# A hybrid decoder block on one core: the borrowed rows of two recurrence gates, copied by ScalarE instead of subtracted by VectorE

## The chip, the cores and the metric

The kernel runs on one core of a Trainium2 chip. The metric is the device time of one execution in microseconds (us), the median of three runs. One further execution was profiled by the hardware; its page and trace are what this document reads.

## The reference, cut to what matters

A block of 512 positions and 1024 channels is computed in float32. One projection `h @ w_in` yields five parts. One part goes through a gated causal convolution of 31 taps, another through a causal convolution of 4 taps, which yields `xb` with 1280 channels, and then through a gated linear recurrence (RG-LRU). Both results are merged, projected and followed by a SwiGLU feed-forward network. The part around the change is the recurrence:

```python
xh = xf.reshape(bsz, s, LRU_HEADS, LRU_BLOCK)          # 16 heads of 80 channels
r = sigmoid(einsum('bshi,hij->bshj', xh, wa).reshape(bsz, s, d) + ba)
i = sigmoid(einsum('bshi,hij->bshj', xh, wx).reshape(bsz, s, d) + bx)
log_a = -LRU_C * r * softplus(-lam)
a, mult = exp(log_a), sqrt(-expm1(2.0 * log_a))
_, h = associative_scan(combine, (a, mult * (i * xf)), axis=1)
```

The 16 heads are 80 channels wide and the tiles of the kernel are 128 channels wide, so a tile of gate outputs needs input rows of a neighbouring tile.

## The kernel before, in words

Channels lie on the 128 partitions and the 512 positions along the free axis. To reach float32 accuracy every matmul operand is split in two: a **rounded part** `h` (a copy into the type fp32r) and a **low part** `l`, which is the value minus `h`. A product is then three matmuls, `h*h`, `h*l` and `l*h`. The helper `split_to` does this: the copy is ScalarE's (L123), the subtraction (the helper `sub`, L119) is VectorE's for activations and GpSimd's for most weights.

Weights arrive in chunks through SyncE's DMA queue; a chunk is loaded some four chunks before TensorE uses it (`AHEAD`), rounded by ScalarE and subtracted by GpSimd into one of five `hl` buffers.

The middle of the kernel follows a list written out by hand (`ORDER`). Its tokens name steps: `u3` (a tile of the gated convolution's input), `rx3` (`xb3` and its split), `g3` (the two gates of tile 3), `r3` (the recurrence of tile 3), `rg3`, `gb3`, `ga3` (other parts of the projection). Between the steps, `run_beside` emits pieces of the long 31-tap convolution, one VectorE instruction per tap and tile (`cv`, L682), which fill VectorE. Within an engine the program then runs in the order that a scheduler settled by its own costs; what is listed below as an order is its outcome.

The step `rx(j)` ends with `ext_in(j)`, which collects the borrowed rows for the gates that need rows of tile j. For gates 0 and 5 (`j5 == 0`) these are the first 32 rows of `xb1` and of `xb6`. They go into a tile `ext` of 96 rows as rounded, low and rounded part, so that one matmul with 96 rows, against weights stacked in the same way, does all three products. ScalarE writes rows 0 to 31 (L782) and 64 to 95 (L783) from `xb`, and VectorE writes rows 32 to 63 by a subtraction (L784, shown in the trace at the helper's line L119). For the other gates, DMAs copy the rows out of the split parts (L789).

The step `gates(j)` (matmuls at L809) multiplies three pairs of the tile's own rows and then, for even `j5`, the one pair with `ext`. In names of the trace, `g` is a bank of gate sums, `z` a bank of the projection, `hl_in` and `hl_gate` split weights, `mu` a bank that the recurrence uses, `ows` sums of weights for a later stage that GpSimd makes in passing, and `y1` a product for the output of the recurrence.

Of the kernel before, what the change touches and what calls it, by code (L numbers as in the profile page):

```python
# [8 lines left out]
F32 = mybir.dt.float32  # L9
# [29 lines left out]
FEW, MANY = 32, 112  # L39
# [47 lines left out]
def tile_block(ctx, tc, a, out):  # L87
# [15 lines left out]
    def pairt(name, dtype=F32R):  # L103

        return longt(f"{name}h", dtype), longt(f"{name}l", dtype)
# [7 lines left out]
    vec, act, pe, pool_e = nc.vector, nc.scalar, nc.tensor, nc.gpsimd  # L113
# [4 lines left out]
    def sub(eng, o, x, y):  # L118
        return eng.tensor_tensor(out=o, in0=x, in1=y, op=ALU.subtract)  # L119
# [505 lines left out]
    ab, e, s, s2, po, c4 = (sm[:, i, :] for i in range(6))  # L625
# [125 lines left out]
    xb, xbp = [], []  # L751

    def rx(j):
        ps = in_mm(RX + j)
        act.activation(ps, ps, AF.Identity, bias=b_in(RX + j))
        o = longt(f"xb{j}")
        lw = lambda s: pc("lru_conv_w", (KL - 1 - s) * NR + j)
        act.activation(o, ps, AF.Identity, scale=lw(0), bias=pc("lru_conv_b", j))
        for s in range(1, KL):
            vec.scalar_tensor_tensor(out=o[:, s:], in0=ps[:, : T - s], scalar=lw(s), in1=o[:, s:], op0=ALU.mult, op1=ALU.add)  # L760
        xb.append(o)
        p_ = pairt(f"xb{j}")
        split(f"xb{j}", o, vec, p_)
        xbp.append(p_)
        ext_in(j)
# [3 lines left out]
    ext = {}  # L769

    def ext_in(i):
        g5, i5 = i - i % 5, i % 5
        for j5 in range(5):
            for at_, nr, tl, r0 in pieces[j5][1]:
                if tl != i5:
                    continue
                key = g5 + j5
                if key not in ext:
                    ext[key] = pairt(f"ext{key}") if j5 % 2 else (longt(f"ext{key}", F32R),)
                if j5 == 0:  # L780
                    full, e = xb[i][:FEW, :], ext[key][0]
                    act.copy(e[:FEW, :], full)  # L782
                    act.copy(e[2 * FEW : 3 * FEW, :], full)  # L783
                    sub(vec, e[FEW : 2 * FEW, :], full, e[:FEW, :].bitcast(F32))  # L784
                    continue
                src = [v[r0 : r0 + nr, :].bitcast(F32) for v in xbp[i]]
                places = [(0, at_, 0), (1, at_, 1)] if j5 % 2 else [(0, at_ + FEW * k, k % 2) for k in range(3)]
                for d, at0, k in places:
                    nc.sync.dma_start(ext[key][d][at0 : at0 + nr, :].bitcast(F32), src[k])  # L789
# [471 lines left out]
```

## Time and profile before

| what | value |
|---|---|
| runs of the kernel | 802.47 us median of 3 (802.31 to 802.84) |
| profiled execution, own time | 803.2 us |
| its span, first to last instruction | 801.4 us |
| granted TensorE clock, mean | 0.998 |
| TensorE matmul busy | 789.4 us, 99% of the span |
| VectorE busy | 677.3 us, 85% |
| ScalarE busy | 471.5 us, 59% |
| GpSimd busy | 232.3 us, 29% |

A row of a timeline reads: start in us, duration in us, engine, line, operation, what is written `<-` what is read, shape, count, and in brackets the idle time of the engine before it with what ended it. PE is TensorE, DVE is VectorE, ACT is ScalarE, POOL is GpSimd, SP is SyncE. The list of waits gives, for an engine and the work that waited, whom it waited for, then total us, times and the longest. The chain that ended last goes back from the last instruction, at each step to what released it.

### The profile page before, as it was taken

The page shows a single profiled execution, that of the slowest core. Times are in us where ns is not written, and L with a number is a line of the kernel's source. Part 1 is how long each engine was busy: PE and PEld are TensorE (multiplying, and loading weights), DVE is VectorE, ACT ScalarE, POOL GpSimd, SP SyncE. Part 2 cuts the span into 40 slices and gives each one's busy share as a digit, 9 for nine tenths or more (in the row PEclk, how much of TensorE's full clock was granted, in tenths as well). Part 3 has the DMA queues.
Part 4 walks back from the last instruction along what each step waited for, and adds up shares of the span by engine and source line. Part 5 has one row for each costly group of instructions (what it writes and reads, how often), then busy time and mean ns, then how long its engine had stood idle before and what let it go on. Part 6 is the DMA issues. An engine that isn't in the chain of part 4 may idle for free.

```text
span 801.4 us, 12193 instructions
## 1 busy us (share of the span) xinstructions
PE 789.4 (99%) x4374; PEld 689.4 (86%) x4374; DVE 677.3 (85%) x1029; ACT 471.5 (59%) x676; POOL 232.3 (29%) x182
## 2 busy tenths in 40 slices
PE   8999999999999999999999999999999999999997
PEld 7988888788888888888888888999999999888885
DVE  4699999999989988795897889977878887889756
ACT  7546585888668864572335574555455555577443
POOL 3565867686865855130000000000000000000000
PEclk9999999999999999999999999999999999999999
DMA  6946556477564664358948536477655553676652
GB/s 207 242 122 166 163 160 198 128 219 209 169 201 145 194 201 140 116 186 265 287 159 249 172 107 183 113 177 185 159 132 133 133 132 104 202 266 204 197 171 105
DMA packets 184624, 140.29 MB, mean 175 GB/s; under 512 B 14279, under 2 KB 162163, under 8 KB 184563
## 3 DMA queue, kind: packets, MB, share of 16 engines
q1 hardware_dynamic: 183123, 134.27, 55.8%
q0 software_dynamic: 1440, 5.24, 3.5%
q8 instruction: 34, 0.56, 0.3%
q14 instruction: 27, 0.22, 0.1%
HBM read 113.79 MB, written 18.64 MB: 165 GB/s over the span
## 4 chain that ended last, share of the span: by engine, by line
PE 84%; DVE 8%; ACT 3%; DMA 2%; issue 1%; POOL 1%; SPq 0%; ACTq 0%; POOLq 0%; DVEq 0%
PE z L523 29%; PE or L935 13%; PE ft L1062 7%; PE yb L523 7%; PE fa L1062 6%; PE ya L523 5%; PE mxr L935 5%; PE fe L1062 3%; PE fr L1062 3%; DVE cv L682 2%; PE fb L1062 2%; PE g L809 2%; PE f L523 1%; DMA raw_fb<-in_ffn_w_dram 1%; DMA raw_in<-in_w_in_dram 1%
## 5 line engine op out<-in xcount | busy, mean ns | idle before, releaser
L682 DVE SCALAR_TENSOR_TENSOR cv<-u,par,cv 128x511 f32<-128x511 f32 (+16 forms) x240 | 162.1, 729 | 2.7 <-ACT cv L679 2.5
L119 POOL TENSOR_TENSOR hl_in<-raw_in,hl_in 128x1024 fp32r<-128x1024 f32 x52 | 126.0, 2429 | 81.3 <-ACT hl_in L123 77.1
L349 POOL DMA_DIRECT2D raw_fb<-raw_fb x10 | 8.7, 875 | 299.7 <-DVE raw_fb L351 186.9
L119 POOL TENSOR_TENSOR ows<-ows 128x256 f32<-128x256 f32 x66 | 57.1, 867 | 37.6 <-DMA ows<-in_ffn_w_dram 34.7
L123 ACT CAST hl_in<-raw_in 128x1024 fp32r<-128x1024 f32 x52 | 54.2, 1043 | 11.5 <-PE z L523 6.6
L123 ACT CAST hl_ft<-raw_fb 128x1024 fp32r<-128x1024 f32 x40 | 41.9, 1049 | 28.5 <-DVE raw_fb L351 12.4
L119 DVE TENSOR_TENSOR hl_ft<-raw_fb,hl_ft 128x1024 fp32r<-128x1024 f32 x40 | 48.6, 1218 | 9.5 <-ACT hl_ft L123 9.4
L119 DVE TENSOR_TENSOR hl_fb<-raw_fb,hl_fb 128x1024 fp32r<-128x1024 f32 x30 | 36.6, 1220 | 8.6 <-ACT hl_fb L123 8.5
L523 PE MATMUL z<-h10h,hl_in 128*128 128x512 f32 (+1 forms) x112 | 42.2, 378 | 1.2 <-DVE h10l L567 1.2
L523 PE MATMUL z<-h16h,hl_in 128*128 128x512 f32 (+1 forms) x112 | 41.7, 374 | 0.0
L523 PE MATMUL z<-h14h,hl_in 128*128 128x512 f32 (+1 forms) x112 | 41.7, 374 | 0.0
L523 PE MATMUL z<-h11h,hl_in 128*128 128x512 f32 (+1 forms) x112 | 41.7, 374 | 0.0
L523 PE MATMUL z<-h13h,hl_in 128*128 128x512 f32 (+1 forms) x112 | 41.7, 374 | 0.0
L523 PE MATMUL z<-h15h,hl_in 128*128 128x512 f32 (+1 forms) x112 | 41.7, 374 | 0.0
L523 PE MATMUL z<-h17h,hl_in 128*128 128x512 f32 (+1 forms) x112 | 41.7, 374 | 0.0
L523 PE MATMUL z<-h12h,hl_in 128*128 128x512 f32 (+1 forms) x112 | 41.7, 374 | 0.0
L351 DVE TENSOR_TENSOR raw_fb<-raw_fb,raw_fb 128x1024 f32<-128x1024 f32 x20 | 24.5, 1224 | 18.0 <-DMA raw_fb<-in_ffn_w_dram 17.6
L119 DVE TENSOR_TENSOR hl_ob<-raw_ob,hl_ob 128x1024 fp32r<-128x1024 f32 (+1 forms) x23 | 27.0, 1174 | 10.2 <-ACT hl_ob L123 10.2
L123 ACT CAST hl_ob<-raw_ob 128x1024 fp32r<-128x1024 f32 (+1 forms) x23 | 23.3, 1013 | 20.9 <-PE or L935 10.8
L123 ACT CAST hl_fb<-raw_fb 128x1024 fp32r<-128x1024 f32 x30 | 31.4, 1046 | 7.0 <-PE mxr L935 3.7
L1062 PE MATMUL fe<-hs_0h,hl_ft 128*128 128x256 f32 x160 | 30.8, 284 | 0.4 <-DVE hl_ft L119 0.4
L1062 PE MATMUL ft<-hs_1h,hl_ft 128*128 128x256 f32 x160 | 30.4, 283 | 0.0
(964 smaller groups left out, 2611.4 us busy)
## 6 DMA issues: line engine op xcount, KB each, us to landing
raw_in<-in_w_in_dram SPq DMA_DIRECT2D x52, 512.0 KB
raw_fb<-in_ffn_w_dram SPq DMA_DIRECT2D x96, 256.0 KB
ows<-in_ffn_w_dram SPq DMA_DIRECT2D x44, 256.0 KB
os<-ows SPq DMA_DIRECT2D x22, 512.0 KB
raw_ob<-in_ffn_w_dram SPq DMA_DIRECT2D x33, 256.0 KB
raw_ot<-os SPq DMA_DIRECT2D x33, 256.0 KB
raw_lo<-in_lru_w_out_dram SPq DMA_DIRECT2D x16, 320.0 KB
raw_fb<-raw_fb POOLq DMA_DIRECT2D x10, 512.0 KB, 4.6
```

The costliest lines, as they stand in the source:

```text
L119: return eng.tensor_tensor(out=o, in0=x, in1=y, op=ALU.subtract)
L123: copy(h, full)
L349: pool_e.dma_start(out=q, in_=y, accum_op=ALU.add)
L351: vec.tensor_tensor(out=q, in0=q, in1=y, op=ALU.add)
L523: pe.matmul(ps, l, r, start=i == 0, stop=i == n - 1)
L682: vec.scalar_tensor_tensor(out=acc[c][:, s:], in0=u[c][:, : T - s], scalar=dw(c, s), in1=acc[c][:, s:], op0=ALU.mult, op1=ALU.add)
L809: pe.matmul(ps, l, r, start=k == 0, stop=k == len(mms) - 1)
L935: pe.matmul(banks[i], l_[:, ts], r_, start=start and n == 0, stop=stop and n == 2, skip_group_check=again)
L1062: pe.matmul(ps[:, HALVES[i]], lw[:, 4 * i + c, :], rx_, start=not (again or i or c or m), stop=bool(i and c == 3 and m == 2), skip_group_c ...
```

## The change

The low part of `xb1` and of `xb6` exists already in full height as `xb1l` and `xb6l` (VectorE's L119 in `rx`). The change takes rows 32 to 63 of `ext` from there by a copy, so VectorE's subtraction of 32 x 512 goes away, twice, and ScalarE has three copies of 32 x 512 in place of two, twice. The two old copies now also read the rounded part `xb1h` or `xb6h` in place of `xb1` or `xb6`.

```diff
                 if j5 == 0:
-                    full, e = xb[i][:FEW, :], ext[key][0]
-                    act.copy(e[:FEW, :], full)
-                    act.copy(e[2 * FEW : 3 * FEW, :], full)
-                    sub(vec, e[FEW : 2 * FEW, :], full, e[:FEW, :].bitcast(F32))
+                    for n, part in enumerate((0, 1, 0)):
+                        act.copy(ext[key][0][FEW * n : FEW * (n + 1), :], xbp[i][part][:FEW, :].bitcast(F32))
                     continue
```

The scheduler answers with another order on VectorE and ScalarE; TensorE's and GpSimd's orders stay as they were. All lines behind the change are two smaller (L847 is L845 now).

On ScalarE, at the rows for gate 5 (`ext_1547`), before:

```order
L123 CAST xb6h<-xb_1538 128x512
L123 CAST hl_in_1620<-raw_in_1618 128x1024
L782 CAST ext_1547<-xb_1538 32x512
L783 CAST ext_1547<-xb_1538 32x512
L123 CAST y1h<-z_1565 128x512
```

and now:

```order
L123 CAST xb6h<-xb_1538 128x512
L123 CAST hl_in_1620<-raw_in_1618 128x1024
L782 CAST ext_1547<-xb6h 32x512
L782 CAST ext_1547<-xb6l 32x512
L782 CAST ext_1547<-xb6h 32x512
L123 CAST y1h<-z_1565 128x512
```

The copy of the low part stands between the other two, behind nothing new; the cast of `y1h` moves back by one row.

On VectorE, some 8 us ahead of that place, at the gate step of tile 4 (`g` and `ea` are its sums and its decay, `cv` two tiles of the convolution), before:

```order
L682 SCALAR_TENSOR_TENSOR cv_1236<-u_875,par,cv_1236 128x490
L682 SCALAR_TENSOR_TENSOR cv_1238<-u_1112,par,cv_1238 128x490
L820 SCALAR_TENSOR_TENSOR g_0_1479<-ea_1492,g_0_1479 128x512
L682 SCALAR_TENSOR_TENSOR cv_1236<-u_875,par,cv_1236 128x489
L822 TENSOR_SCALAR ea_1492<-g_0_1479 128x512
```

and now:

```order
L682 SCALAR_TENSOR_TENSOR cv_1236<-u_875,par,cv_1236 128x490
L682 SCALAR_TENSOR_TENSOR cv_1238<-u_1112,par,cv_1238 128x490
L682 SCALAR_TENSOR_TENSOR cv_1236<-u_875,par,cv_1236 128x489
L818 SCALAR_TENSOR_TENSOR g_0_1479<-ea_1492,g_0_1479 128x512
L682 SCALAR_TENSOR_TENSOR cv_1238<-u_1112,par,cv_1238 128x489
L820 TENSOR_SCALAR ea_1492<-g_0_1479 128x512
```

One more tap of the convolution stands ahead of the gate step. Most steps between gate 0 and here have moved back by one tap in the same way.

On VectorE, at the split of `xb6` and the subtraction that goes (`mu` and the L833 rows belong to the recurrences of tiles 2 and 3, `z_1565` becomes `y1`), before:

```order
L833 SCALAR_TENSOR_TENSOR xb_779<-ea_1196,mu_1606 128x512
L832 TENSOR_TENSOR mu_1613<-xb_943,mu_1613 128x512
L119 TENSOR_TENSOR xb6l<-xb_1538,xb6h 128x512
L847 TENSOR_TENSOR z_1565<-xb_681,z_1565 128x512
L833 SCALAR_TENSOR_TENSOR xb_943<-ea_1369,mu_1613 128x512
L119 TENSOR_TENSOR ext_1547<-xb_1538,ext_1547 32x512
L119 TENSOR_TENSOR y1l<-z_1565,y1h 128x512
```

and now:

```order
L831 SCALAR_TENSOR_TENSOR xb_779<-ea_1196,mu_1606 128x512
L845 TENSOR_TENSOR z_1565<-xb_681,z_1565 128x512
L119 TENSOR_TENSOR xb6l<-xb_1538,xb6h 128x512
L830 TENSOR_TENSOR mu_1613<-xb_943,mu_1613 128x512
L682 SCALAR_TENSOR_TENSOR cv_1238<-u_1112,par,cv_1238 128x488
L831 SCALAR_TENSOR_TENSOR xb_943<-ea_1369,mu_1613 128x512
L682 SCALAR_TENSOR_TENSOR cv_1236<-u_875,par,cv_1236 128x487
L119 TENSOR_TENSOR y1l<-z_1565,y1h 128x512
```

`z_1565` stands ahead of `xb6l` in place of `mu_1613`, the subtraction into `ext_1547` is gone, and two taps have moved in. Likewise, in the step of tile 5, the product that becomes `y0` now stands ahead of `xb5l` and not behind it.

At gate 0 ScalarE's rows change in the same way as at gate 5, but there both copies of the rounded part stand first and the copy of the low part last, directly ahead of the sigmoid into `sgb` (L840 before).

## The prediction

> **What bounds the kernel now.** The page first, for which engine fills the span; then TensorE's own waits; then the chain that ended last, to see whether time won at a wait lasts to the end.
>
> ```profile
> span 801.4 us, 12193 instructions
> PE 789.4 (99%) x4374; PEld 689.4 (86%) x4374; DVE 677.3 (85%) x1029; ACT 471.5 (59%) x676; POOL 232.3 (29%) x182
> ```
>
> TensorE is busy for 789.4 of 801.4 us. A change off TensorE can win only where TensorE waits, 12.0 us in all. This is the list of those waits:
>
> ```profile
> PE g L809 <- DVE ext L119: 1.2, 1, 1.2
> ...
> PE fe L1062 <- DVE hl_ft L119: 0.4, 1, 0.4
> PE f L523 <- ACT h20h L566: 0.4, 1, 0.4
> PE th L563 <- DVE h24l L567: 0.3, 1, 0.3
> ```
>
> The longest single wait is for `ext`, the tile that the change makes in another way. It happens once, so at one of the two gates. TensorE's timeline shows where:
>
> ```profile
> 159.01 0.39 PE L809 MATMUL g<-xb5l,hl_gate 128*128 128x512 f32 x1
> 159.24 0.39 PE L809 MATMUL g<-xb5h,hl_gate 128*128 128x512 f32 x1
> 160.84 0.47 PE L809 MATMUL g<-ext,hl_gate 96*128 96x512 f32 x1 [1.21 <-DVE ext L119]
> ```
>
> It is gate 5. Matmuls start 0.22 to 0.23 us apart (159.01 to 159.24), so the one with `ext` would have started at 159.46; it started at 160.84. The wait costs 1.38 us, more than the 1.21 in brackets, because those leave out the overlap of two matmuls. The chain that ended last, in order of time:
>
> ```profile
> 158.96 1.75 DVE ext L119
> 160.84 1.40 PE g L809 x5
> ...
> 458.31 0.91 PE th L563 x8
> ...
> 504.97 4.69 DMA raw_fb<-raw_fb
> ...
> 517.30 0.74 PE fe L1062 x4
> ```
>
> The subtraction stands in that chain, and from 160.84 to 458 there is nothing but TensorE. From 461 to 517 VectorE, ScalarE and DMAs alternate, then TensorE again.
>
> **Gate 5, what goes and what comes.** These are VectorE's rows up to the wait:
>
> ```profile
> 148.65 0.70 DVE L820 SCALAR_TENSOR_TENSOR g<-ea,g 128x512 f32<-128x512 f32 x1 [0.28 <-ACT g L819]
> 149.26 0.73 DVE L682 SCALAR_TENSOR_TENSOR cv<-u,par,cv 128x489 f32<-128x489 f32 x1
> 149.89 0.69 DVE L822 TENSOR_SCALAR ea<-g 128x512 f32<-128x512 f32 x1
> ...
> 154.73 1.21 DVE L833 TENSOR_TENSOR_SCAN xb<-ea,mu 128x512 f32<-128x512 f32 x1
> ...
> 156.44 0.76 DVE L119 TENSOR_TENSOR xb6l<-xb,xb6h 128x512 fp32r<-128x512 f32 x1
> 157.12 0.68 DVE L847 TENSOR_TENSOR z<-xb,z 128x512 f32<-128x512 f32 x1
> 157.72 1.21 DVE L833 TENSOR_TENSOR_SCAN xb<-ea,mu 128x512 f32<-128x512 f32 x1
> 158.96 1.74 DVE L119 TENSOR_TENSOR ext<-xb,ext 32x512 fp32r<-32x512 f32 x1
> ```
>
> The subtraction into `ext` stood behind a product and a scan, and then took 1.74 us; it ended at 160.70 and TensorE started 0.14 later. `xb6l`, which holds the same numbers, was done at 157.20. ScalarE's rows:
>
> ```profile
> 155.70 0.61 ACT L123 CAST xb6h<-xb 128x512 fp32r<-128x512 f32 x1
> 156.21 1.05 ACT L123 CAST hl_in<-raw_in 128x1024 fp32r<-128x1024 f32 x1
> 157.16 0.61 ACT L782 CAST ext<-xb 32x512 fp32r<-32x512 f32 x1
> 157.79 0.62 ACT L783 CAST ext<-xb 32x512 fp32r<-32x512 f32 x1
> ...
> 158.92 1.05 ACT L123 CAST hl_in<-raw_in 128x1024 fp32r<-128x1024 f32 x1
> ```
>
> Two copies of this shape start 0.63 apart (157.16, 157.79). Three, from the same place, start at 157.16, 157.79 and 158.42 and end at 159.04; with the 0.14 from end to matmul, TensorE could start at 159.18. It arrives at 159.46. The wait is gone with 0.28 to spare, if `xb6l` is there for the second copy at 157.79.
>
> Is it? The new order puts one more convolution tap ahead of the gate step at 148.65. A tap costs 0.63 (149.26 to 149.89) and the step waited 0.28 for ScalarE, so it comes 0.35 later, and so does everything behind it: the last add of `xb6`, which ends where the scan at 154.73 starts, ends at 155.1, early enough for ScalarE's `xb6h` at 155.70. Then the scan (at most 1.21), `z` 0.60 (157.12 to 157.72) and `xb6l` 0.68 to 0.76 give 157.5 to 157.7, against 157.79 needed. Further upstream the new order also moves single taps, but VectorE's `xb4l` follows ScalarE's `xb4h`, whose place is set by ScalarE:
>
> ```profile
> 110.22 0.61 ACT L123 CAST xb4h<-xb 128x512 fp32r<-128x512 f32 x1
> ```
>
> ```profile
> 110.86 2.46 DVE L119 TENSOR_TENSOR xb4l<-xb,xb4h 128x512 fp32r<-128x512 f32 x1
> ```
>
> That sets VectorE's clock anew at 110.86; from there the moved rows stand at most one tap, 0.65, later, until `xb5l` and the product for `y0`, where the two orders have done the same rows. `ext` is ready between 158.4 (if ScalarE runs 0.6 earlier, since the product that it waits for, `y0`'s, now comes one row of 0.6 sooner) and 159.2 (if `xb6l` is done 0.1 late); I take 159.04, the value of the rows as they stand.
>
> What waits on ScalarE behind the added copy: `y1h` and the next weight cast, 0.63 later. GpSimd takes that weight only after the one before:
>
> ```profile
> 156.73 1.07 POOL L119 TENSOR_TENSOR ows<-ows 128x256 f32<-128x256 f32 x1
> 157.76 5.21 POOL L119 TENSOR_TENSOR hl_in<-raw_in,hl_in 128x1024 fp32r<-128x1024 f32 x2
> ```
>
> Two subtractions in 5.21 us: the second starts near 160.2, and its cast ended at 159.97 (158.92 + 1.05), and with the added copy at 160.6, so at worst GpSimd is 0.4 late with a weight that is loaded four chunks ahead of its use. I cost it at nothing; its cover is that lead, and without it the 0.4 would be TensorE's.
>
> **Gate 0.** The same edit at an earlier place:
>
> ```profile
> 60.77 0.62 ACT L783 CAST ext<-xb 32x512 fp32r<-32x512 f32 x1
> 61.42 0.69 ACT L840 ACTIVATE sgb<-z,par 128x512 f32<-128x512 f32 x1
> ...
> 66.31 0.62 ACT L123 CAST hl_gate<-raw_gate 128x512 fp32r<-128x512 f32 x1 [2.02 <-POOL hl_in L119]
> ```
>
> ```profile
> 60.72 1.13 DVE L119 TENSOR_TENSOR xb1l<-xb,xb1h 128x512 fp32r<-128x512 f32 x1
> ...
> 101.41 4.08 DVE L682 SCALAR_TENSOR_TENSOR cv<-u,par,cv 128x511 f32<-128x511 f32 x6 [1.69 <-ACT cv L679]
> ```
>
> ```profile
> 72.19 0.40 PE L809 MATMUL g<-ext,hl_gate 96*128 96x512 f32 x1
> ```
>
> Here the copy of the low part is last and waits for `xb1l`, done at 61.85; it runs to about 62.6. TensorE needs it at 72.19: 9.6 us to spare. The sigmoid at 61.42 and the rows behind it come 1.15 later, and ScalarE's idle 2.02 ahead of 66.31 takes that up. VectorE is rid of a subtraction that freed at most the 1.74 of its twin, and loses the gain in its idle 1.69 at 101.41. Value: zero.
>
> **The sum.** 1.38 us less at gate 5, zero elsewhere. After it, TensorE's work is the same and runs 1.38 earlier; VectorE, relieved of 1.75 us with two or three taps more already done, is ahead by at least as much. The stretch from 461 to 517 begins with TensorE's transposes (`th`, 458.31) and hangs on what they release, so it moves along. The profiled execution, 803.2 with a span of 801.4, would become 801.8; it is 0.7 above the median of the runs, so against the median: 802.47 - 1.38 = **801.1 us**, 0.17% less.
>
> **A rule weighed.** The subtraction into `ext` took 1.74 although only 32 rows high, and `xb4l` at 110.86 took 2.46. GpSimd at that time:
>
> ```profile
> 110.39 2.39 POOL L119 TENSOR_TENSOR hl_in<-raw_in,hl_in 128x1024 fp32r<-128x1024 f32 x1 [4.28 <-ACT hl_in L123]
> ```
>
> Both began inside a GpSimd subtraction and ended 0.5 to 0.6 us after it (112.78 to 113.32 here, about 160.1 to 160.70 there): VectorE was held until GpSimd was through. An undisturbed one of 128 x 512:
>
> ```profile
> 143.35 0.68 DVE L119 TENSOR_TENSOR xb5l<-xb,xb5h 128x512 fp32r<-128x512 f32 x1
> ```
>
> [...]
>
> **The rivals.** First, *the wait stays on the other side* (slower). If `xb6l` starts after GpSimd's `hl_in` (157.76) it is held as `xb4l` was: until 160.3, plus 0.68 is 161.0, then two copies of 0.63 and 0.2 for handovers: TensorE starts at 162.5 instead of 160.84, 1.65 us worse, **804.1 us**. It decides from a start of `xb6l` about 1.0 us later than the 156.8 worked out. For it speaks the case at 110.86; against it that GpSimd's `hl_in` needs ScalarE's cast, which stands behind `xb6h`, so a late VectorE makes GpSimd late too. Chance 0.06.
>
> Second, *part of the wait remains*: the same hold, but by a short `ows` row (1.07 at 156.73), or an `xb5l` that loses the race which it won before:
>
> ```profile
> 143.25 3.04 POOL L119 TENSOR_TENSOR hl_in<-raw_in,hl_in 128x1024 fp32r<-128x1024 f32 x1 [6.08 <-ACT hl_in L123]
> ```
>
> `xb5l` began 0.10 behind this row and took its 0.68, and GpSimd's took 3.04 instead of 2.4. Were VectorE the one held, it would come 1.7 late, and TensorE would start near 160.8 as now. Wins of 0 to 0.8: **801.7 to 802.5 us**. Chance 0.17.
>
> Third, *the time is given back*: TensorE arrives earlier, but one of the DMAs between 461 and 517 (4.69 us at 504.97) is not released earlier, and the 0.4 at `fe` grows to 1.8. **802.4 us**. For it: the chain there isn't TensorE's. Against: every link starts from a release that TensorE began. Chance 0.11.
>
> Fourth, *more is won*: the waits of 0.4, 0.4 and 0.3 shrink also because VectorE is ahead. At most 1.38 + 1.1: **800.0 us**. Chance 0.08.
>
> **How the numbers follow.** The forecast, 800.7 to 801.5, has 0.58. About 0.2% is what a measurement of this kernel can tell from no change, 1.6 us here. Faster than that: the fourth rival and a fifth or so of the forecast's spread, 0.21. Slower: the first, 0.06. Within: the rest, 0.73. The range takes in the forecast, most of the second and third and the nearer half of the fourth: 800.3 to 802.5.
>
> **What would show it.** Right: no wait of TensorE for `ext`; the first `ext` matmul of gate 5 0.23 us behind the one before; three copies on ScalarE ending near 159; the matmuls at 458 about 1.4 us earlier. Wrong: a wait of `g` for ScalarE, `xb6l` or `xb5l` above 1.5 us, or a wait at `fe` that has grown by what was won.

## The result, and the profile after

| | before | changed |
|---|---|---|
| median of 22 runs each, side by side | 802.62 us (801.51 to 803.68) | 801.43 us (800.02 to 802.61) |
| profiled execution, span | 801.4 us | 799.2 us |

The ratio is 0.9982, with a 95% interval of 0.9976 to 0.9987: 1.4 us less, between 1.0 and 1.9. The forecast was 801.1, 1.38 less. Where a later comparison gives a ratio, it stands against the kernel before on the chip of that comparison, whose median was 803.2 to 803.3 there.

TensorE's waits in the changed kernel, the longest first:

```profile
PE warm L495 <- DVE ones L488: 1.1, 1, 1.1
PE z L523 <- DVE h10l L567: 1.0, 1, 1.0
PE tx L563 <- DVE x L579: 0.9, 2, 0.6
PE fe L1060 <- DVE hl_ft L119: 0.4, 1, 0.4
PE f L523 <- ACT h20h L566: 0.4, 1, 0.4
```

The wait for `ext` is gone, and no other has taken its place: `fe` and `f` have their 0.4 as before, and the 0.3 of `th` is not in this profile. TensorE at gate 5:

```profile
158.82 0.39 PE L807 MATMUL g<-xb5h,hl_gate 128*128 128x512 f32 x1
159.05 0.40 PE L807 MATMUL g<-ext,hl_gate 96*128 96x512 f32 x1
```

The matmul with `ext` follows 0.23 behind the one before; it was 1.60 (159.24 to 160.84). That is 1.37 us. The chain that ended last, with the rows that answer to those before:

```profile
71.25 1.85 PE g L807 x8
...
158.53 1.85 PE g L807 x8
160.38 21.78 PE z L523 x96
...
456.22 0.87 PE th L563 x8
...
502.72 4.65 DMA raw_fb<-raw_fb
...
515.04 0.74 PE fe L1060 x4
```

In the kernel before, the first of these rows read:

```profile
71.67 1.85 PE g L809 x8
```

So this execution was 0.42 ahead already at gate 0. That comes from the start-up and not from the change: in the chains of the experiments below that pass it, the same row stands between 71.42 and 71.76 with the change at gate 0, and between 71.16 and 72.19 without it. The two profiles have to be compared with that shift. `th` comes at 456.22 instead of 458.31, 2.09 earlier: 0.42 of the start, 1.37 of gate 5, 0.3 in between. `fe` comes at 515.04 instead of 517.30, 2.26 earlier: behind 458 nothing is given back. So the spans of these two executions differ by 2.2, of which 1.37 is the wait at gate 5; over all executions the medians differ by 1.2.

ScalarE at gate 5 now:

```profile
155.49 1.05 ACT L123 CAST hl_in<-raw_in 128x1024 fp32r<-128x1024 f32 x1
156.44 0.61 ACT L782 CAST ext<-xb6h 32x512 fp32r<-32x512 f32 x1
157.19 0.62 ACT L782 CAST ext<-xb6l 32x512 fp32r<-32x512 f32 x1
157.83 0.62 ACT L782 CAST ext<-xb6h 32x512 fp32r<-32x512 f32 x1
158.47 0.59 ACT L123 CAST y1h<-z 128x512 fp32r<-128x512 f32 x1
```

and VectorE, with GpSimd beside it:

```profile
148.58 0.69 DVE L818 SCALAR_TENSOR_TENSOR g<-ea,g 128x512 f32<-128x512 f32 x1
...
156.37 0.80 DVE L119 TENSOR_TENSOR xb6l<-xb,xb6h 128x512 fp32r<-128x512 f32 x1
```

```profile
156.62 2.79 POOL L119 TENSOR_TENSOR hl_in<-raw_in,hl_in 128x1024 fp32r<-128x1024 f32 x1
```

The copies end at 158.45; with 0.14 to the matmul, TensorE could have started at 158.59 and arrived at 159.05, 0.46 to spare. The copy of the low part started 0.14 behind the end of the first instead of 0.02, since `xb6l` was done only at 157.17. And `xb6l` began 0.25 ahead of GpSimd's `hl_in`, which then took 2.79 instead of 2.4: GpSimd was the one held.

### The profile page after: what moved, and what is told of

It is laid out like the page before. It is cut to its first block, busy times and chain, and to the rows that moved or that the text cites. A ratio compares the mean times of both kernels' runs of the same rounds, so it can differ in the third digit from the quotient of the medians.

```text
span 799.2 us, 12191 instructions
## 1 busy us (share of the span) xinstructions
PE 788.9 (99%) x4374; PEld 689.5 (86%) x4374; DVE 675.5 (85%) x1027; ACT 472.1 (59%) x678; POOL 231.6 (29%) x182
## 4 chain that ended last, share of the span: by engine, by line
PE 91%; DVE 4%; DMA 2%; ACT 2%; issue 1%; SPq 0%; DVEq 0%; POOLq 0%; ACTq 0%
PE z L523 35%; PE or L933 13%; PE ft L1060 7%; PE yb L523 7%; PE fa L1060 6%; PE ya L523 5%; PE mxr L933 5%; PE fe L1060 3%; PE g L807 3%; PE fr L1060 3%; PE fb L1060 2%; PE f L523 1%; DMA raw_fb<-in_ffn_w_dram 1%; DMA raw_fb<-raw_fb 1%; DMA x<-in_x_dram 1%
## 5 line engine op out<-in xcount | busy, mean ns | idle before, releaser
L119 POOL TENSOR_TENSOR hl_in<-raw_in,hl_in 128x1024 fp32r<-128x1024 f32 x52 | 125.9, 2426 | 82.8 <-ACT hl_in L123 80.4
L119 POOL TENSOR_TENSOR ows<-ows 128x256 f32<-128x256 f32 x66 | 57.2, 870 | 37.5 <-DMA ows<-in_ffn_w_dram 34.5
L119 DVE TENSOR_TENSOR hl_ft<-raw_fb,hl_ft 128x1024 fp32r<-128x1024 f32 x40 | 48.6, 1219 | 9.7 <-ACT hl_ft L123 9.6
L119 DVE TENSOR_TENSOR hl_fb<-raw_fb,hl_fb 128x1024 fp32r<-128x1024 f32 x30 | 36.6, 1220 | 9.2 <-ACT hl_fb L123 8.9
L523 PE MATMUL z<-h10h,hl_in 128*128 128x512 f32 (+1 forms) x112 | 42.2, 378 | 1.0 <-DVE h10l L567 1.0
L523 PE MATMUL z<-h13h,hl_in 128*128 128x512 f32 (+1 forms) x112 | 41.7, 374 | 0.0
L523 PE MATMUL z<-h14h,hl_in 128*128 128x512 f32 (+1 forms) x112 | 41.7, 374 | 0.0
L523 PE MATMUL z<-h15h,hl_in 128*128 128x512 f32 (+1 forms) x112 | 41.7, 374 | 0.0
L523 PE MATMUL z<-h11h,hl_in 128*128 128x512 f32 (+1 forms) x112 | 41.7, 374 | 0.0
L523 PE MATMUL z<-h16h,hl_in 128*128 128x512 f32 (+1 forms) x112 | 41.7, 374 | 0.0
L523 PE MATMUL z<-h17h,hl_in 128*128 128x512 f32 (+1 forms) x112 | 41.7, 374 | 0.0
L523 PE MATMUL z<-h12h,hl_in 128*128 128x512 f32 (+1 forms) x112 | 41.7, 374 | 0.0
L119 DVE TENSOR_TENSOR hl_ob<-raw_ob,hl_ob 128x1024 fp32r<-128x1024 f32 (+1 forms) x23 | 27.0, 1172 | 10.5 <-ACT hl_ob L123 7.6
```

The costliest lines, as they stand in the source:

```text
L523: pe.matmul(ps, l, r, start=i == 0, stop=i == n - 1)
```

## The experiments

The theory: what counts is when `ext` is ready against TensorE's arrival at gate 5; before, VectorE's subtraction made it late, mostly because GpSimd held it. The rival: the gain comes from the work taken from VectorE and the other order of its taps. In each, the wait is given as the step from the matmul before to the one with `ext`, less the usual 0.23.

**One gate at a time.** The kernel before with the change under a condition:

```diff
                 if j5 == 0:
+                    if key == 5:
+                        for n, part in enumerate((0, 1, 0)):
+                            act.copy(ext[key][0][FEW * n : FEW * (n + 1), :], xbp[i][part][:FEW, :].bitcast(F32))
+                    else:
                         full, e = xb[i][:FEW, :], ext[key][0]
...
```

> The change at gate 5 alone; gate 0 keeps its subtraction. Theory (all of the gain is TensorE's wait of 1.38 us at gate 5): no wait of TensorE for ext, and about 1.4 us less than before (ratio 0.9982). Rival (VectorE's relief by two subtractions and the other order of its taps): about half of the gain, 0.6 to 0.7 us, since one of two subtractions goes.

Measured: 0.9985 (0.9976 to 0.9994), 1.2 us less, and no wait of TensorE for `ext`. One gate alone has, as measured, the gain of both; but the interval goes from 0.5 to 1.9 us, so the rival's 0.6 to 0.7 is not ruled out by the time alone. In its profile a small wait stands at the next gate instead:

```profile
183.96 0.47 PE L813 MATMUL g<-ext6h,hl_gate 112*128 112x512 f32 x1 [0.18 <-DMA ext6h<-xb7h]
184.64 0.47 PE L813 MATMUL g<-ext6l,hl_gate 112*128 112x512 f32 x1 [0.21 <-DMA ext6l<-xb7l]
```

The other half has `key == 0` in the condition.

> The change at gate 0 alone; gate 5 keeps its subtraction, but the scheduler now puts it one row earlier, ahead of the scan and not behind it. Theory that the hold by GpSimd set the end of this subtraction: it starts about 1 us earlier, inside the GpSimd subtraction hl_in, is held until that is through and ends near 160.0 as before; TensorE waits 0.7 to 1.4 us and the time falls by 0 to 0.7 us. Rival (the place in VectorE's queue set it): it ends a scan (1.1 us) earlier, TensorE's wait falls to 0.2 to 0.3 us and the time by 1.1 us, with gate 5 untouched.

Measured: 0.9996 (0.9988 to 1.0005), no gain that can be told; the theory's 0 to 0.7 us holds it, the rival's 1.1 lies just outside the interval (at most 1.0 less). At gate 5 its profile shows what the subtraction does one row earlier in VectorE's queue:

```profile
157.12 0.68 DVE L836 TENSOR_TENSOR mu<-xb,mu 128x512 f32<-128x512 f32 x1
157.83 2.17 DVE L119 TENSOR_TENSOR ext<-xb,ext 32x512 fp32r<-32x512 f32 x1
160.03 1.22 DVE L837 TENSOR_TENSOR_SCAN xb<-ea,mu 128x512 f32<-128x512 f32 x1
```

```profile
156.65 5.62 POOL L119 TENSOR_TENSOR hl_in<-raw_in,hl_in 128x1024 fp32r<-128x1024 f32 x2
```

It started at 157.83, ahead of the scan, and took 2.17 instead of 1.74: it ended at 160.00 in place of 160.70. TensorE waited 1.07 (158.84 to 160.14, less 0.23). Standing a scan earlier in the queue brought 0.3 of the 1.1 that its place alone would give. The hold by GpSimd set the end.

**The hold taken away.** The kernel before, where the low part of one weight chunk (`gb3`) is left out, so that GpSimd does not subtract at that time; the rounded part is used in its place.

```diff
-            h, l = split_to(hl[:, 0, :n], hl[:, 1, :n], rv, lo)
+            if key == "in47":
+                h = l = hl[:, 0, :n]
+                act.copy(h, rv)
+            else:
+                h, l = split_to(hl[:, 0, :n], hl[:, 1, :n], rv, lo)
```

> The kernel before, but the low part of one weight chunk (gb3, the GpSimd subtraction at 157.76) is left out, and the rounded part is used in its place. Theory (VectorE's subtraction into ext took 1.74 us because GpSimd's ran): it takes about 0.68, ends 1.06 earlier, and TensorE waits 0.3 instead of 1.38; about 1.1 us less than before. Rival (it takes 1.74 by itself, since its rows 32 to 63 read and write across partitions): the duration stays 1.74 and the wait 1.38; no change of time.

Measured: 0.9987 (0.9978 to 0.9996), 1.0 us less (0.3 to 1.8) where 1.1 was worked out. VectorE's order is that of before:

```profile
157.78 1.21 DVE L837 TENSOR_TENSOR_SCAN xb<-ea,mu 128x512 f32<-128x512 f32 x1
159.02 0.68 DVE L119 TENSOR_TENSOR ext<-xb,ext 32x512 fp32r<-32x512 f32 x1
```

```profile
159.29 0.39 PE L813 MATMUL g<-xb5h,hl_gate 128*128 128x512 f32 x1
159.85 0.47 PE L813 MATMUL g<-ext,hl_gate 96*128 96x512 f32 x1 [0.17 <-DVE ext L119]
```

The same subtraction, at the same place behind the scan, takes 0.68 and not 1.74, and the wait falls from 1.38 to 0.33. So of the 1.38 us that the change wins, 1.06 were GpSimd's hold and 0.3 the place behind the scan. Rows 32 to 63 as such cost nothing more.

**The low part copied by VectorE.** The changed kernel with

```diff
                     for n, part in enumerate((0, 1, 0)):
-                        act.copy(ext[key][0][FEW * n : FEW * (n + 1), :], xbp[i][part][:FEW, :].bitcast(F32))
+                        copy = vec.tensor_copy if part else act.copy
+                        copy(ext[key][0][FEW * n : FEW * (n + 1), :], xbp[i][part][:FEW, :].bitcast(F32))
```

> The changed kernel, but the low part's copy into ext is VectorE's, with one input, at both gates. The scheduler puts it behind the scan again, and GpSimd's weight cast ahead of xb6h on ScalarE. Theory (what counts is when ext is ready; a subtraction of VectorE that begins inside GpSimd's is held): xb6l begins after GpSimd's hl_in, takes 2 us or more, ext is ready near 161, TensorE waits 1.5 to 2.3 us, and the time is 0 to 0.9 us above before. Rival (what counts is that the subtraction with two inputs goes from VectorE): no wait above 0.3 us and 1 us or more less than before.

Measured: 1.0020 (1.0010 to 1.0030), 1.6 us slower than before, more than the 0 to 0.9 expected. VectorE, GpSimd and TensorE:

```profile
156.62 2.14 DVE L119 TENSOR_TENSOR xb6l<-xb,xb6h 128x512 fp32r<-128x512 f32 x1
158.68 1.21 DVE L832 TENSOR_TENSOR_SCAN xb<-ea,mu 128x512 f32<-128x512 f32 x1
159.92 1.35 DVE L783 CAST ext<-xb6l 32x512 fp32r<-32x512 f32 x1
```

```profile
155.81 2.41 POOL L119 TENSOR_TENSOR hl_in<-raw_in,hl_in 128x1024 fp32r<-128x1024 f32 x1
158.56 2.42 POOL L119 TENSOR_TENSOR hl_in<-raw_in,hl_in 128x1024 fp32r<-128x1024 f32 x1 [0.35 <-ACT hl_in L123]
```

```profile
159.06 0.39 PE L808 MATMUL g<-xb5h,hl_gate 128*128 128x512 f32 x1
161.41 0.47 PE L808 MATMUL g<-ext,hl_gate 96*128 96x512 f32 x1 [1.97 <-ACT hl_in L123]
```

The subtraction with two inputs into `ext` is gone from VectorE, as in the change, and the time rises: the rival falls. GpSimd's `hl_in` began first this time, `xb6l` was held (2.14), the copy with one input after it was held too (1.35), and TensorE waited 2.12, 0.74 more than before. At gate 0, where GpSimd ran nothing beside it, the same copy took 0.42:

```profile
62.97 0.42 DVE L783 CAST ext<-xb1l 32x512 fp32r<-32x512 f32 x1
```

(The bracket at the matmul names a weight cast of ScalarE that ran until 161.43, so it did not release the matmul; ScalarE's two copies into `ext` were done at 156.93. The copy on VectorE ended at 161.27, 0.14 ahead of the matmul.) This is the first rival of the prediction, seen on the chip. What the profiled execution lost beside the 0.74 shows in the run with four copies, below.

**More copies on ScalarE.** The changed kernel, with rows 64 to 95 of gate 5's `ext` written again once, twice or four times:

```diff
-                    for n, part in enumerate((0, 1, 0)):
+                    for n, part in [(0, 0), (1, 1), (2, 0)] + [(2, 0)] * (1 if key else 0):
```

> The changed kernel with one copy of 32 x 512 more at gate 5 (rows 64 to 95 are written twice); the scheduler puts it behind the cast of y1h. From the changed kernel's rows ext is then ready at 158.98 + 0.62 + 0.14 = 159.74, TensorE arrives at 159.05. Theory (the moment at which ext is ready is all that counts): TensorE waits 0.7 us, and the time lies 0.7 us above the changed kernel, some 0.7 below before. Rival (what won was the work taken from VectorE): no change against the changed kernel.

Measured: 0.9985 (0.9975 to 0.9994). TensorE waited 0.82:

```profile
159.35 0.62 ACT L782 CAST ext<-xb6h 32x512 fp32r<-32x512 f32 x1
```

```profile
159.06 0.39 PE L807 MATMUL g<-xb5h,hl_gate 128*128 128x512 f32 x1
160.11 0.47 PE L807 MATMUL g<-ext,hl_gate 96*128 96x512 f32 x1 [0.66 <-ACT ext L782]
...
184.80 0.47 PE L807 MATMUL g<-ext6h,hl_gate 112*128 112x512 f32 x1 [0.78 <-DMA ext6h<-xb7h]
```

159.35 + 0.62 + 0.14 is 160.11, the start of the matmul: the wait follows the last copy. Whether the time lies 0.7 above the changed kernel, the interval (1.5 us wide) does not tell.

> The same with two copies more, the second behind a weight cast. ext is ready near 161.35, so TensorE waits 2.3 us. Theory: 2.3 us above the changed kernel, 0.9 us above before; if a wait above 2 us always makes TensorE's granted clock fall, as it did after the wait of 2.1 us in the run with VectorE's copy, 1.6 us more, 2.5 us above before. Rival: no change against the changed kernel.

Measured: 1.0014 (1.0004 to 1.0025), 1.1 us above before where 0.9 was worked out; the wait was 2.52 (158.99 to 161.74, less 0.23). Behind it, in the profiled execution, the granted clock did not fall (1.00 from 160 to 185 us):

```profile
161.74 1.40 PE g L807 x5
184.92 2.75 PE g L807 x12
```

From gate 5 to gate 6 it took 23.18, as before (160.84 to 184.02). But the ten executions lie in two groups: six took 803.4 to 804.1 us, the profiled one among them, and four took 804.7 to 806.5. The step of about 2 us is near what a fall of the clock costs in the next run, 1.61 us, so the fall may have come in some of the four; none of them was profiled, and this is not shown. If it did, the 1.1 is a mixture, and its closeness to 0.9 is in part chance. The twelve executions with VectorE's copy spread likewise, four from 803.2 to 803.6 and eight from 804.3 to 806.4.

> The same with four copies more. ext is ready near 162.6, TensorE waits 3.5 us. Theory: 3.5 us in the profile at this place, and again a fall of the granted clock behind it if the length of the wait decides it. Rival: no wait that lasts.

One execution, 807.07 us; the wait was 3.80. Here, and in the run with VectorE's copy, TensorE went on slower a little after the wait. Its rows with four copies:

```profile
164.00 0.40 PE L807 MATMUL g<-ext,hl_gate 96*128 96x512 f32 x1
164.23 0.53 PE L523 MATMUL z<-h10h,hl_in 128*128 128x512 f32 x1
164.56 0.63 PE L523 MATMUL z<-h10l,hl_in 128*128 128x512 f32 x1
...
167.54 0.50 PE L523 MATMUL z<-h12h,hl_in 128*128 128x512 f32 x1
167.88 0.39 PE L523 MATMUL z<-h13h,hl_in 128*128 128x512 f32 x1
```

Eight matmuls stand 0.43 apart instead of 0.23. From gate 5 to gate 6 it took 24.79 (162.99 to 187.78), 1.61 more than 23.18; with VectorE's copy 24.74 (161.43 to 186.17), 1.56 more. That is the second part of the loss in that run's profiled execution, 805.32 us.

**Other places in the order.** In two profiles above TensorE waited at gate 6 for a DMA into `ext6`. The changed kernel with gate 6 one place later:

```diff
-        gb3 rg2 rx8 g6 rg3 u6 r4 r5 g7
+        gb3 rg2 rx8 rg3 g6 u6 r4 r5 g7
```

> The changed kernel with the step g6 one place later in the order (behind rg3), so that TensorE does 24 matmuls, 5.4 us, more ahead of gate 6. In two experiments TensorE waited 0.4 and 0.8 us at gate 6 for a DMA into ext6 that took 5.3 and 6.1 us; in the profile of the changed kernel it didn't. Theory (that DMA lands just in time, and in some executions late): no wait at gate 6, and the time 0 to 0.5 us below the changed kernel, 1.4 to 1.9 below before. Rival (the DMA is not near the limit in the changed kernel): the same as the changed kernel, or slower if the later gate shows up as a wait elsewhere.

Measured: 0.9986 (0.9977 to 0.9995), the same as the changed kernel. No wait at gate 6 in its profile, but there was none in the changed kernel's either. Whether that DMA costs something in some executions stays open.

The kernel before, subtraction and all, with gate 5 one place later:

```diff
-        ... u5 g5 rx7
+        ... u5 rx7 g5
```

> The kernel before, with its subtraction, but the step g5 behind rx7, so that TensorE does 24 matmuls, 5.4 us, more ahead of gate 5. Theory (only the meeting of ext and TensorE counts): the subtraction may stay as long as it was, TensorE no longer waits for ext, and the time falls by 1.4 us as with the change. Rival (work taken from VectorE is what wins): VectorE's work is the same, so the time stays.

Measured: 1.0022 (1.0012 to 1.0031), 1.8 us slower. The first half of the theory's forecast came, the second did not:

```profile
PE z L523 <- ACT sg L744: 1.0, 1, 1.0
PE g L809 <- DMA ext<-xb8l: 0.8, 1, 0.8
PE z L523 <- DVE xb L821: 0.7, 1, 0.7
```

TensorE no longer waited for `ext` of gate 5, but 2.5 us in three new places: for a sigmoid, for a DMA into the rows of gate 7, and for VectorE's step that reads a gate's sums (L821). So the meeting of `ext` and TensorE could be mended from TensorE's side too, but in the one order tried the waits only moved elsewhere. Both stated outcomes missed: the time did not fall by 1.4, and it did not stay. Among these kernels none beats the changed one.

## Why the prediction was right

**The wait as the only term.** Forecast 1.38; the profile shows 1.37 at that place, gate 5 alone gives 0.9985 and gate 0 alone 0.9996. The run without GpSimd's subtraction gains 1.0 us with VectorE's work and order as before, and the run with VectorE's copy loses although the subtraction is gone: it is the wait, and not the work taken from VectorE. Right.

**When `ext` is ready.** With the 0.42 of the start added back, the forecast's moments can be set beside the chip's. VectorE's gate step 0.35 later: 148.58 + 0.42 is 149.00, against 148.65 + 0.35. `xb6l` at 156.8: 156.79. TensorE at 159.46: 159.47. The last copy's end was put at 159.04, between 158.4 and 159.2: it was 158.87, because ScalarE ran 0.3 earlier than before, the lower bound's reason at half its size. The margin was 0.46 instead of 0.28.

**Gate 0 at nothing.** Right: the copy of the low part waited 0.4 for `xb1l` on ScalarE, and TensorE for neither.

```profile
61.47 0.62 ACT L782 CAST ext<-xb1l 32x512 fp32r<-32x512 f32 x1 [0.38 <-DVE xb1l L119]
```

**The time kept to the end.** Right: `fe` kept its wait of 0.4 and moved along. The third rival is out for this execution. Of the fourth, the wait of 0.3 at `th` is missing here, which is most of the 0.3 gained in between; in the profiles with two copies more and with gate 6 later it is there, 0.3 and 0.2, so it is not shown to be the change's doing.

**The first rival's distance was mis-sized.** The prediction had it decide from a start of `xb6l` about 1.0 us later, because it left GpSimd's `hl_in` at 157.8. In the changed kernel GpSimd began it at 156.62 (157.04 with the start's 0.42), since ScalarE's cast ended earlier and the short `ows` rows were done sooner, and `xb6l` was ahead by 0.25 only. In the runs with one, two and four copies more, GpSimd's `hl_in` came as early (156.75 to 156.86) and the lead was 0.25, 0.27 and 0.25, and none of the 22 executions of the changed kernel came near 804.1. In the kernel before, a subtraction 0.10 behind GpSimd's still ran (`xb5l`, 0.68) and one 0.47 behind was held (`xb4l`, 2.46); so, as an estimate from these two rows, the hold would have come with 0.35 to 0.72 us more, and not with 1.0. The forecast held with less room than it claimed, and to that extent by luck. The argument that a late VectorE makes GpSimd late too holds only while `xb6h` stands ahead of that cast on ScalarE; in the run with VectorE's copy the scheduler had them the other way round, and the rival happened. (There the cast began at 154.09 and `xb6h` at 155.03.) Its price was put at 1.65 above before; that run paid 0.74 in the wait, less because GpSimd was through by 158.2 and not by 160.3, and 1.56 in the clock, which the prediction did not know of. The second rival is out for this execution: `xb5l` began 0.05 behind GpSimd's row and took 0.69.

**The second subtraction's length.** The hold was read from two rows, 1.74 and 2.46 against 0.68. The run without GpSimd's subtraction shows it: 0.68 at the same place. Two inputs are not needed for it: in the run with VectorE's copy, the 32 x 512 copy with a single input took 1.35 us inside GpSimd's subtraction, and 0.42 at gate 0. ScalarE's copies were not held: the two that began inside GpSimd's `hl_in` at gate 5 of the changed kernel took 0.62 each. Why VectorE waits for GpSimd, no trace here shows.

## What to carry to other kernels

Where one engine is busy 99% of the span, read its list of waits: a single wait of 1.2 us can be the whole prize, and the step between two neighbouring starts, less the usual step, gives its price. Look at a row's duration as well as its place in the queue: the same operation at 0.68 and at 1.74 says that something held it, and taking the other party away shows who. A copy moved to an idle engine pays if what it reads is made early, and then that earlier row inherits the risk.

## What the runs showed of the hardware that had not been expected

A wait of TensorE can cost a second time. Behind the wait of 2.12 us (VectorE's copy) and the one of 3.80 (four copies more) TensorE did seven or eight matmuls at 0.43 us instead of 0.23 each, 1.56 and 1.61 us more in all. Its granted clock was 0.74 from 160 to 165 us behind the first, and 0.72 from 165 to 170 us behind the second. Behind a wait of 2.52 (two copies more), and behind the 1.38 of the kernel before, it was 1.00 from 160 to 170 us. Each is one profiled execution. So the length of the wait alone does not decide, and what does stays open.

Which of VectorE and GpSimd was held was settled, in these rows, within half a microsecond. In the changed kernel `xb6l` 0.25 ahead of `hl_in` took 0.80, and GpSimd paid 0.4; `xb5l`, before, began 0.10 behind and still took its 0.68, and GpSimd paid 0.64; `xb4l`, before, began 0.47 behind and took 2.46. That row, `xb4l` and `xb9l` of the changed kernel and `xb6l` of the run with VectorE's copy began 0.47 to 1.54 us into a single GpSimd subtraction of 128 x 1024. All four were held: they took 1.40 to 2.46 and ended 0.54 after it.

Not every subtraction of VectorE was held. The one that makes `y3l` reads `y3h` and a bank of the projection, which the matmuls of L523 write; the kernel places the banks in PSUM (L94), and `xb` and the split parts in SBUF. In the kernel before it ran inside a GpSimd subtraction and took its 0.69:

```profile
197.38 0.69 DVE L119 TENSOR_TENSOR y3l<-z,y3h 128x512 fp32r<-128x512 f32 x1
```

```profile
196.52 2.40 POOL L119 TENSOR_TENSOR hl_in<-raw_in,hl_in 128x1024 fp32r<-128x1024 f32 x1 [0.53 <-ACT hl_in L123]
```

In the kernel before and the changed one, seven subtractions of this kind began 0.44 to 1.93 us into a single GpSimd subtraction of that size, and all took 0.68 or 0.69. So of the subtractions above that began 0.44 us or more into GpSimd's, those that were held read both inputs from SBUF, as the one into `ext` does, and those that were not held read one from PSUM. Whether that is the cause, no run shows.
